# Two transformer blocks on one core: a ring of expert weights with 20 buffers instead of 18, and another order of its buffers and of the second block's first loads

## The chip, the core and the metric

The program runs on one core of a Trainium2 chip. Its time is device microseconds of one execution; the median of three runs of the kernel before is 1735.8 us (1735.76 to 1737.29). The engines of the core are TensorE (PE, with its weight loads shown as PEld), VectorE (DVE), ScalarE (ACT), GpSimd (POOL) and SyncE (SP), which here does little else than issue DMAs.

## The reference

256 tokens of width 1024 go through two blocks. The first projects the tokens, runs a causal convolution of width 31 and a gated linear attention, mixes both, and then a mixture of experts: a router takes one of 8 groups and two of its 8 experts for each token. The second block has four branches (a recurrent mixer, window means, a sparse attention, an attention over 256 memory tokens) and a gated feed-forward part. The part around the change is the mixture of experts:

```
e_logits = logits of the chosen group; top 2 of 8, softmax, times the group's weight
hdn = silu(xb @ w1[e]) * (xb @ w3[e])        # xb: the tokens of expert e, w1 and w3: 1024 x 512
y   = hdn @ w2[e]                            # w2: 512 x 1024
out = sum over the two experts of weight * y # 64 experts, f32 throughout
```

All 64 experts are computed, each for the tokens that chose it.

## The kernel before

Everything is one program, and a planner (the tile framework, with `schedule_with_timeline_sim=True`, L1681) writes the order of the instructions on each engine from a time that it simulates; in a few stretches the order of some engines is that of the source (`manual_schedule`). Weights come as pieces of 128 x 2048 f32, 1 MB or 8 KB a partition, all issued by SP in program order (L139).

*The first block* (`first`, `first_in`, `first_out`) reads its pieces through the pool `wp` of three buffers. ACT copies each piece to a rounded `hi` (L170), DVE and POOL compute the rest `lo` (L172, L173), and PE multiplies three times (L186 to L188). Its tiles that live long (gates, convolution, the pool `keep1`) lie on the right side of the memory.

*The experts* (`Experts`, `experts`) are computed in 32 pairs. A pair needs 12 pieces: w1 and w3 of both experts in halves (8), then w2 in halves (4). Two pieces for the memory tokens' keys and values come after pair 6 (`mem_at`). The class `Experts` deals the loads out over a ring of buffers that belong to several pools: `wq0` (3), `wq1` (3), `wp` (3), `lo` (3) and `wq2` (6), 18 in all; in the first round three buffers of `hi` come behind them, so 21 loads are issued before a buffer has to come back. A load waits until the last reader of its buffer is done; SP issues in order, so what stands behind it waits too. `wq0` and `wq1` open while the first block still runs, `wq2` when `keep1` is closed.

One pair (`block`) is: 32 gathers of the tokens with one-hot matrices (L786), one copy (L789), the product with w1 and w3 (L796, 64 instructions), a copy and four transposes (L799, L802), silu and product (L807, L808), the product with w2 (L815, 32), two copies and eight accumulating matmuls (L865). The gathers of the next pair do not depend on this one, and the planner mixes them into L815. Behind pair 3 stands a loop for experts with over 32 tokens (`overflow`), behind pair 6 the projection of the memory tokens (`memory_kv`). A small pool `mid` on the right side holds that projection's results.

*The second block* (`second`) starts with a layer norm of the experts' sum, which needs two rows of parameters (`ln2`, loaded into a `lo` buffer, read by L263 and L267) and a gain (`gain`, read by L1071). Its SP queue is written out (L1043 to L1053): one piece of weights, ln2, gain, two more pieces, then five tables. Tiles of this block lie on the right side, where `wq2` was.

Of the kernel before, what the change touches and what calls it, by code (L numbers as in the profile page):

```python
# [8 lines left out]
F32 = mybir.dt.float32  # L9
# [8 lines left out]
P = 128  # L18
T = 256
# [109 lines left out]
class Stream:  # L129


    def __init__(self, nc, pool):
        self.nc, self.pool = nc, pool
# [136 lines left out]
def first(tc, A, k):  # L270
    nc = tc.nc
    ps, x1, st = k.ps, k.x1, k.stream
    ident, ones = k.cav("ident"), k.cav("ones")
    V, S, G = nc.vector, nc.scalar, nc.gpsimd

    def bank(shape=(P, 512)):
        return ps.tile(list(shape), F32, tag="ps", name="pst", bufs=k.n_ps)

    def mx(shape=(P, 512)):
        return ps.tile(list(shape), F32, tag="mx", name="mxt", bufs=8 - k.n_ps)  # L280

    st.open([A["s1"][i] for i in range(A["s1"].shape[0])])
    sp = Split(nc, k.hi, k.lo)
    dn = Dense(k, sp, st.take, bank)
    tail = ExitStack()
    with ExitStack() as es:
        bp = es.enter_context(tc.tile_pool(name="keep1", bufs=1, side="right"))
        kept = {n: bp.tile([P, NB, T], F32, tag=n, name=n) for n in ("lk", "vn", "g1", "g0", "cv")}
        kept.update({n: bp.tile([P, NB, T], F32R, tag=n, name=n) for n in ("oh", "ol")})
        cols = bp.tile([P, NCOLS1], F32, name="cols")  # L290

        def col(name, j=0):
            return cols[:, COLS1[name][0] + j:COLS1[name][0] + j + 1]

        with ExitStack() as es2:
            tp = es2.enter_context(tc.tile_pool(name="tmp1", bufs=2, side="right"))
            ap = es2.enter_context(tc.tile_pool(name="act1", bufs=1, side="right"))
            early = es2.enter_context(ExitStack())
            first_in(tc, A, k, dn, sp, bank, mx, kept, cols, col, bp, ap, tp, early)
        sp.cut = PIECE * 5 // 8  # L300
        k.experts.open("wq1", k.n_q1)
        ap = tail.enter_context(tc.tile_pool(name="tail", reuse_waits="tile", bufs=1))
        rows = ap.tile([P, NROWS1 - 1536], F32, name="rows")
        nc.scalar.dma_start(rows[:], A["rows1"][:, 1536:].to_broadcast([P, NROWS1 - 1536]))
        wrt = ap.tile([P, NB, 72], F32, name="wrt")
        nc.scalar.dma_start(wrt[:], A["wrt"])

        def row(name):
            a, b = ROWS1[name]
            return rows[:, a - 1536:b - 1536]  # L310

        r = Route(tc, k, ap, mx, wrt, row("b_rt"))
        first_out(tc, A, k, dn, sp, bank, kept, col, row, bp, ap, r.logits)
    k.open_mid()
    k.experts.open("wq2", k.n_q2, "right")
    k.experts.ahead(k.experts.depth)
    with tail:
        r.choose()
# [402 lines left out]
class Experts:  # L721


    def __init__(self, tc, A, k, es):
        self.tc, self.k, self.es = tc, k, es
        self.w1, self.w3, self.w2 = A["w1"][0], A["w3"][0], A["w2"][0]
        loads = self.loads = []
        for pr in range(32):
            for kh in range(2):
                for e in (2 * pr, 2 * pr + 1):  # L730
                    loads += [(("1", e, kh), self.half(self.w1[e], kh)), (("3", e, kh), self.half(self.w3[e], kh))]
            for jh in range(2):
                for e in (2 * pr, 2 * pr + 1):
                    loads.append((("2", e, jh), self.half(self.w2[e], jh)))
            if pr == k.mem_at:
                loads += [(("m", 0, kh), A["wm"][kh]) for kh in range(2)]
        self.index = {key: i for i, (key, _) in enumerate(loads)}
        self.got, self.at = {}, 0
        self.pools = {"wp": k.wp, "lo": k.lo, "hi": k.hi}
        ring = ["wq0"] * k.n_q0 + ["wq1"] * k.n_q1 + ["wp"] * k.n_wp + ["lo"] * k.n_lo + ["wq2"] * k.n_q2  # L740
        self.depth = len(ring) + k.n_hi
        self.order = ring + ["hi"] * k.n_hi + ring * (len(loads) // len(ring))

# [270 lines left out]
def second(tc, A, k, out):  # L1014
    nc = tc.nc
# [5 lines left out]
    st_ = k.stream  # L1021
# [8 lines left out]
    with ExitStack() as es:  # L1030
# [12 lines left out]
        with tc.manual_schedule(engines={mybir.EngineType.SP}):  # L1043
            st_.ahead(1)
            ln2 = st_.load(A["rows2"][:, :2 * D].to_broadcast([P, 2 * D]), k.lo)
            ln2 = ln2[:].rearrange("p (a d) -> p a d", a=2)
            nc.sync.dma_start(gain[:], A["rows2"][:, 4 * D:5 * D].to_broadcast([P, D]))
            st_.ahead(3)
            nc.sync.dma_start(cr, A["const_h"].rearrange("p (a b) -> p a b", a=4))
            nc.sync.dma_start(cl[:], A["const_l"].rearrange("p (m t) -> p m t", m=7))  # L1050
            nc.sync.dma_start(cpm[:], A["const_p"])
            nc.sync.dma_start(cb[:], A["const_b"])
            nc.sync.dma_start(pw[:], A["pool_wl"])  # L1053
# [457 lines left out]
def body(tc, A, out):  # L1511
    nc = tc.nc
    k = K()
    k.n_hi, k.n_lo, k.n_wp, k.n_ps = 3, 3, 3, 4
    k.n_q0, k.n_q1, k.n_q2 = 3, 3, 6
    k.loop_at = 4
    k.mem_at = 6
    with ExitStack() as es:
        cp = es.enter_context(tc.tile_pool(name="const", bufs=1))
        k.hi = es.enter_context(tc.tile_pool(name="hi", bufs=k.n_hi))  # L1520
        k.lo = es.enter_context(tc.tile_pool(name="lo", bufs=k.n_lo))
        k.wp = es.enter_context(tc.tile_pool(name="wp", bufs=k.n_wp))
        k.ps = es.enter_context(tc.tile_pool(name="psum", bufs=4, space=PSUM))
        k.stream = Stream(nc, k.wp)
        k.ca = cp.tile([P, NCA], F32, name="ca")
        k.cav = lambda n: k.ca[:, CA[n][0]:CA[n][1]]
        k.eps_ln = cp.tile([P, 1], F32, name="eps_ln")
        k.eps_rms = cp.tile([P, 1], F32, name="eps_rms")
        nc.vector.memset(k.eps_ln[:], LN_EPS)
        nc.vector.memset(k.eps_rms[:], RMS_EPS)  # L1530
        k.x1 = cp.tile([P, 2, D], F32, name="x1")
        k.am = cp.tile([P, 2, 64], BF16, name="am")
        k.counts = cp.tile([P, 2, P], BF16, name="counts")
        k.W = cp.tile([P, 2, 64], F32, name="Wt")
        k.pos = cp.tile([P, 2, 64], F32, name="pos")
        k.ovn = cp.tile([P, 64], F32, name="ovn")
        k.ovs = cp.tile([P, 64], F32, name="ovs")
        k.n_extra = cp.tile([1, 1], I32, name="n_extra")
        k.count = cp.tile([P, 1], F32, name="count")
        k.cols2 = cp.tile([P, NCOLS2], F32, name="cols2")  # L1540
        k.col2 = lambda n, j=0: k.cols2[:, COLS2[n][0] + j:COLS2[n][0] + j + 1]
        nc.vector.memset(k.count[:], 0.0)
        with ExitStack() as mid:
            rings = mid.enter_context(ExitStack())

            def open_mid():
                pool = mid0.enter_context(tc.tile_pool(name="mid", reuse_waits="tile", bufs=1, side="right"))
                k.mid = pool
                k.mkT = pool.tile([P, 2, T], F32, name="mkT")
                k.mv = pool.tile([P, 2, T], F32, name="mv")  # L1550
                k.lb = pool.tile([P, 2, 4], F32, name="lb")
                k.lbm = pool.tile([P, 2, 4], F32, name="lbm")

            mid0 = es.enter_context(ExitStack())
            k.open_mid = open_mid
            k.experts = Experts(tc, A, k, rings)
            first(tc, A, k)
            nc.scalar.dma_start(k.cols2[:], A["cols2"])
            experts(tc, A, k)
        k.stream.open([A["s2"][i] for i in range(A["s2"].shape[0])])  # L1560
        second(tc, A, k, out)


# [121 lines left out]
```

## Time and profile before

| | |
|---|---|
| median of three runs | 1735.8 us |
| profiled execution | 1743.47 us, span 1741.7 us |
| PE busy | 1621.3 us, 93% |
| PEld busy | 1120.6 us, 64% |
| DVE, ACT, POOL busy | 553.3, 461.8, 491.9 us |
| moved by DMA | 533.20 MB, 306 GB/s over the span |
| expert loads | 384 of 1 MB, all issued by SP, 19.4 us median from issue to landing |

Engine busy times count the stretch from an instruction's start to its end; matmul ends are modelled. "Share" of the DMA is the mean over 16 DMA engines. PEclk is the clock that TensorE was granted, as a share of 2.4 GHz.

### The profile page before, as it was taken

To read this page: it belongs to the slowest core of one execution; us is meant where nothing else is said; L and a number is where in the kernel's file an instruction comes from. 1 tells how busy PE (TensorE), PEld (TensorE's weight loads), DVE (VectorE), ACT (ScalarE), POOL (GpSimd) and SP (SyncE) were. 2 spreads that over 40 slices of the span, in tenths; PEclk is the share of its full clock that TensorE was granted. 3 is DMA by queue.
4 is the path that set the end of the run, shared out by engine and by line. 5 is a ranking of instruction groups with operands and counts; after the bars stand their busy time and mean duration, and the time that the engine had idled before them with its cause. 6 is when DMAs were issued, how large, how long until landed. Compare 5 with 4: busy or idle time off the path is not lost. (4 is left out here: it accounts for less than half of the span.)

```text
span 1741.7 us, 23653 instructions
## 1 busy us (share of the span) xinstructions
PE 1621.3 (93%) x9895; PEld 1120.6 (64%) x9895; DVE 553.3 (32%) x1034; ACT 461.8 (27%) x618; POOL 491.9 (28%) x338
## 2 busy tenths in 40 slices
PE   8999998999899999999999999999699998979998
PEld 7999995445455444444354434444399997979997
DVE  5888684110110000000000000000563866453233
ACT  6445751100200000000000000000356544454333
POOL 6767742000000000000000000000354454556664
PEclk9999996898898997787877787787899998989999
DMA  7453678999989999999999999999544332535551
GB/s 272 162 181 140 250 282 326 426 412 425 426 365 417 426 427 426 426 426 426 426 426 426 426 426 426 426 426 416 190 155 161 113 131 97 182 121 191 177 188 73
DMA packets 75694, 533.20 MB, mean 306 GB/s; under 512 B 8497, under 2 KB 9009, under 8 KB 11970
## 3 DMA queue, kind: packets, MB, share of 16 engines
q1 hardware_dynamic: 74178, 526.61, 74.7%
q10 hardware_dynamic: 1408, 5.06, 0.7%
q8 instruction: 79, 1.29, 0.3%
q14 instruction: 29, 0.24, 0.0%
HBM read 530.59 MB, written 1.05 MB: 305 GB/s over the span
## 5 line engine op out<-in xcount | busy, mean ns | idle before, releaser
L173 POOL TENSOR_TENSOR lo<-w,hi 128x768 fp32r<-128x768 f32 (+2 forms) x112 | 379.2, 3391 | 353.6 <-ACT hi L170 253.7
L786 PEld LDWEIGHTS pst<-S,x 128*128 128x128 f32 x1024 | 249.3, 334 | 80.1 <-issue 78.7
L170 ACT ACTIVATE hi<-w 128x2048 fp32r<-128x2048 f32 (+1 forms) x112 | 208.9, 1868 | 224.1 <-PE pst L187 123.1
L796 PE MATMUL pst<-w,xe 128*32 128x512 f32 x2048 | 267.3, 612 | 1.1 <-DVE xe L789 1.1
L815 PE MATMUL pst<-w,hd 128*32 128x512 f32 x1024 | 245.6, 893 | 24.4 <-DVE hd L808 24.4
L841 POOL TENSOR_TENSOR sw<-S,Wt 128x64 f32<-128x64 f32 x128 | 33.3, 292 | 827.3 <-DVE S L851 546.4
L786 PE MATMUL pst<-S,x 128*128 128x64 f32 x1024 | 261.3, 421 | 1.5 <-DVE S L851 1.2
L187 PE MATMUL pst<-ul,hi 128*128 128x256 f32 x768 | 218.4, 285 | 0.0
L188 PE MATMUL pst<-uh,lo 128*128 128x256 f32 x768 | 217.9, 285 | 0.3 <-DVE lo L172 0.3
L186 PE MATMUL pst<-uh,hi 128*128 128x256 f32 x768 | 217.5, 284 | 0.0
L796 PEld LDWEIGHTS pst<-w,xe 128*32 128x32 f32 x2048 | 70.3, 113 | 167.2 <-issue 160.0
L172 DVE TENSOR_TENSOR lo<-w,hi 128x1280 fp32r<-128x1280 f32 (+1 forms) x78 | 124.4, 1595 | 157.0 <-ACT hi L170 148.7
L186 PEld LDWEIGHTS pst<-uh,hi 128*128 128x128 f32 x768 | 145.9, 190 | 1.7 <-ACT il L1152 0.3
L188 PEld LDWEIGHTS pst<-uh,lo 128*128 128x128 f32 x768 | 145.0, 189 | 2.1 <-DVE lo L172 0.9
L187 PEld LDWEIGHTS pst<-ul,hi 128*128 128x128 f32 x768 | 145.1, 189 | 1.8 <-issue 0.5
L808 DVE TENSOR_TENSOR hd<-si,pst 128x128 f32<-128x128 f32 x64 | 18.5, 288 | 377.6 <-ACT si L807 377.6
L789 DVE COPY xe<-pst 128x512 f32<-128x512 f32 x32 | 22.1, 692 | 340.2 <-PE pst L786 340.2
L815 PEld LDWEIGHTS pst<-w,hd 128*32 128x32 f32 x1024 | 42.3, 141 | 120.1 <-issue 80.1
L845 ACT ACTIVATE WT<-pst 128x256 f32<-128x256 f32 x32 | 12.3, 384 | 400.5 <-PE pst L843 383.9
L368 DVE SCALAR_TENSOR_TENSOR mxt<-U,cols,mxt 128x256 f32<-128x256 f32 x232 | 113.2, 488 | 6.9
L865 PE MATMUL acc<-ys,WT 64*128 64x512 f32 x256 | 89.2, 694 | 16.4 <-DVE ys L823 16.4
L186 PE MATMUL pst<-xh,hi 128*128 128x256 f32 x352 | 98.8, 284 | 6.1 <-ACT hi L170 6.0
(399 smaller groups left out, 2054.9 us busy)
## 6 DMA issues: line engine op xcount, KB each, us to landing
w<-in_w_dram SPq DMA_DIRECT2D x384, 1024.0 KB, 19.4
w<-in_s_dram SPq DMA_DIRECT2D x108, 1024.0 KB, 4.8
w<-in_wm_dram SPq DMA_DIRECT2D x2, 1024.0 KB, 19.5
rows<-in_rows_dram ACTq DMA_DIRECT2D x1, 1572.0 KB
w<-in_s_dram SPq DMA_DIRECT2D x4, 256.0 KB, 6.7
xn<-in_x_dram ACTq DMA_DIRECT2D x1, 1024.0 KB, 9.0
mem<-in_mem_dram ACTq DMA_DIRECT2D x1, 1024.0 KB, 11.2
w<-in_rows_dram SPq DMA_DIRECT2D x1, 1024.0 KB, 9.1
```

Source lines behind the costliest of these rows:

```text
L170: nc.scalar.activation(hi[:, s], raw[:, s], AF.Copy)
L172: nc.vector.tensor_tensor(lo[:, v], raw[:, v], hf[:, v], op=OP.subtract)
L173: nc.gpsimd.tensor_tensor(lo[:, g], raw[:, g], hf[:, g], op=OP.subtract)
L186: mm(out, lh, rh, start=start and c == 0, stop=False, skip_group_check=True)
L187: mm(out, lh, rl, start=False, stop=False, skip_group_check=True)
L188: mm(out, ll, rh, start=False, stop=stop and c == n - 1, skip_group_check=True)
L368: V.scalar_tensor_tensor(cv[:, blk] if j == 30 else acc, U[:, blk, j:j + T], cols[:, cw + j:cw + j + 1], acc, op0=OP.mult, op1=OP.add)
L786: nc.tensor.matmul(pg[:, c], x1[:, t, c::NB], Sx[:, t], start=t == 0, stop=t == 1)
L796: nc.tensor.matmul(ph[g:g + 32, :], xe[:, c, e * CAP:(e + 1) * CAP], w[:, c % 4, :], start=c == 0, stop=c == NB - 1)
L815: nc.tensor.matmul(py[g:g + 32, :], hd[:, j, e], w[:, j % 2, half * 512:half * 512 + 512], start=j == 0, stop=j == 3)
L841: G.tensor_tensor(sw[:, t, dup, :m].rearrange("p (e s) -> p e s", e=n), Sx[:, t].rearrange("p (e s) -> p e s", e=n), wts[t], op=OP.mult)
L865: nc.tensor.matmul(acc[t][half][:], wt_, y, start=pr == 0, stop=pr == 31, skip_group_check=True)
```

## The change

The ring has 20 buffers. `wq2` has eight instead of six, and four of them stand ahead of `wp` and `lo` in the order of the ring, so that 23 loads are issued in the first round. The place in memory comes from the scratch kept for dynamic DMAs, which is set to 1024 bytes, and the four tiles of the pool `mid` go into the constants' pool; `open_mid` goes away. In the second block's SP queue two pieces of weights are issued ahead of the gain instead of behind it.

```diff
-    k.open_mid()
     k.experts.open("wq2", k.n_q2, "right")
...
-        ring = ["wq0"] * k.n_q0 + ["wq1"] * k.n_q1 + ["wp"] * k.n_wp + ["lo"] * k.n_lo + ["wq2"] * k.n_q2
+        ring = (["wq0"] * k.n_q0 + ["wq1"] * k.n_q1 + ["wq2"] * 4 + ["wp"] * k.n_wp + ["lo"] * k.n_lo
+                + ["wq2"] * (k.n_q2 - 4))
         self.depth = len(ring) + k.n_hi
...
+            st_.ahead(3)
             nc.sync.dma_start(gain[:], A["rows2"][:, 4 * D:5 * D].to_broadcast([P, D]))
-            st_.ahead(3)
...
-    k.n_q0, k.n_q1, k.n_q2 = 3, 3, 6
+    k.n_q0, k.n_q1, k.n_q2 = 3, 3, 8
...
+        k.mkT = cp.tile([P, 2, T], F32, name="mkT")
+        k.mv = cp.tile([P, 2, T], F32, name="mv")
+        k.lb = cp.tile([P, 2, 4], F32, name="lb")
+        k.lbm = cp.tile([P, 2, 4], F32, name="lbm")
...
-    nc = bacc.Bacc("TRN2", target_bir_lowering=False, num_devices=1)
+    nc = bacc.Bacc("TRN2", target_bir_lowering=False, num_devices=1, dynamic_dma_scratch_size=1024)
```

## Rows read from the trace of the kernel before

**Rows 1.** The page: the span, and GB/s moved in 40 equal slices.

```profile
span 1741.7 us, 23653 instructions
...
GB/s 272 162 181 140 250 282 326 426 412 425 426 365 417 426 427 426 426 426 426 426 426 426 426 426 426 426 426 416 190 155 161 113 131 97 182 121 191 177 188 73
```

**Rows 2.** Windows by pair: start:end, length, busy by engine (count), PEclk, DMA share, GB/s.

```profile
358.60:383.90 25.30, 23.73 (x146) 12.36 (x142) 2.41 (x6) 2.13 (x5) 1.04 (x4) 0.93 1.01 425
...
415.90:444.30 28.40, 26.05 (x142) 13.14 (x142) 4.54 (x14) 6.45 (x16) 1.04 (x4) 0.94 1.01 426
...
520.30:550.80 30.50, 27.77 (x142) 13.27 (x142) 2.22 (x6) 2.13 (x5) 1.04 (x4) 0.83 1.00 414
550.80:575.00 24.20, 22.69 (x142) 12.18 (x142) 2.22 (x6) 2.13 (x5) 1.04 (x4) 1.00 1.01 426
...
599.30:627.80 28.50, 26.21 (x142) 13.14 (x142) 2.22 (x6) 2.13 (x5) 1.04 (x4) 0.88 1.01 424
...
656.20:687.00 30.80, 28.48 (x142) 13.82 (x142) 2.22 (x6) 2.13 (x5) 1.04 (x4) 0.72 1.01 426
...
656.20:1195.60 539.40, 501.30 (x2556) 239.84 (x2556) 39.66 (x106) 38.31 (x90) 17.74 (x68) 0.79 1.01 426
```

**Rows 3.** Waits of PEld, whole span: line, releaser, us in total, times, longest.

```profile
PEld pst L796 <- DMA w<-in_w_dram: 4.2, 8, 1.1
...
PEld pst L815 <- DMA w<-in_w_dram: 1.2, 4, 0.3
```

**Rows 4.** Waits of the SP queue, whole span.

```profile
SPq L139 <- DMA w<-in_w_dram: 475.8, 249, 2.8
...
SPq L139 <- PE pst L796: 175.0, 59, 19.4
```

**Rows 5.** Windows, columns as in rows 2: stretches in which the DMA slows down.

```profile
250.00:262.00 12.00, 12.00 (x61) 10.03 (x60) 9.05 (x11) 5.62 (x5) 6.21 (x2) 1.00 0.57 186
...
292.00:302.00 10.00, 9.64 (x52) 4.78 (x55) 0.96 (x3) 0.38 (x1) 1.04 (x4) 0.57 0.39 162
...
510.00:515.00 5.00, 4.64 (x23) 1.10 (x26) 0.96 (x3) 0.38 (x1) 1.04 (x4) 0.50 0.48 198
515.00:520.00 5.00, 5.00 (x48) 1.28 (x40) 0.00 (x0) 0.00 (x0) 0.00 (x0) 0.94 0.42 125
```

**Rows 6.** Timeline of PE in a pair of 24.2 us: start, us, instruction.

```profile
558.47 1.92 PE L815 MATMUL pst<-w,hd 128*32 128x512 f32 x16
560.33 1.16 PE L786 MATMUL pst<-S,x 128*128 128x64 f32 x4
```

**Rows 7.** Timeline of PE in a pair of 30.8 us.

```profile
663.90 3.64 PE L815 MATMUL pst<-w,hd 128*32 128x512 f32 x16
667.48 3.60 PE L786 MATMUL pst<-S,x 128*128 128x64 f32 x14
```

**Rows 8.** Timeline of DVE at the end of the first block.

```profile
258.48 2.06 DVE L179 TENSOR_TENSOR ml<-g,mh 128x256 fp32r<-128x256 f32 x1
```

**Rows 9.** Timeline of PE: the first expert product.

```profile
296.01 9.32 PE L796 MATMUL pst<-w,xe 128*32 128x512 f32 x64 [0.35 <-DVE xe L789]
```

**Rows 10.** Timeline of the SP queue where the second block begins.

```profile
1214.43 0.33 SPq L139 DMA_DIRECT2D w<-in_rows_dram  x1
1232.11 0.33 SPq L1047 DMA_DIRECT2D gain<-in_rows_dram  x1
```

**Rows 11.** Timeline of all engines there.

```profile
1219.17 7.07 PE L796 MATMUL pst<-w,xe 128*32 128x512 f32 x62
...
1236.31 1.41 DVE L263 SCALAR_TENSOR_TENSOR x<-acc,lmv,w 128x512 f32<-128x512 f32 x2
...
1244.47 1.97 PE L1010 MATMUL mxt<-ca,un 128*128 128x128 f32 x8 [8.32 <-DVE un L1071]
...
1252.67 3.90 DVE L1000 TENSOR_TENSOR rss<-rss 128x1 f32<-128x1 f32 x1 [0.79 <-ACT un L994]
```

**Rows 12.** DMA issues: queue, count, KB, median us to landing.

```profile
w<-in_rows_dram SPq DMA_DIRECT2D x1, 1024.0 KB, 9.1
```

More of the change, by code (lines that the diff above doesn't have):

```diff
@@ L1542, in body @@
         nc.vector.memset(k.count[:], 0.0)
+        k.mkT = cp.tile([P, 2, T], F32, name="mkT")
+        k.mv = cp.tile([P, 2, T], F32, name="mv")
+        k.lb = cp.tile([P, 2, 4], F32, name="lb")
+        k.lbm = cp.tile([P, 2, 4], F32, name="lbm")
         with ExitStack() as mid:
             rings = mid.enter_context(ExitStack())
[L1546 to L1555, printed above, removed]
             k.experts = Experts(tc, A, k, rings)
```

## The prediction

> **What bounds the kernel now.** I read the page's span and DMA rate by slices first: from the eighth to the 28th of 40 slices the rate stands at 412 to 427 GB/s, and once at 365 [rows 1]. That is the expert stage, 384 loads of 1 MB. So I asked next for the same stage pair by pair, from the end of one pair's L796 to the end of the next's [rows 2] (they are pairs 3, 5, 8, 9, 11 and 13, and the 18 pairs from 13 to 30). The reader is to see two things that do not fit together at first sight: the DMA share is 1.01, and PE is busy 501.30 of 539.40 us. Twelve loads of 1.0486 MB at 426 GB/s need 29.5 us; the 18 pairs took 539.4 / 18 = 29.97 us each. Both look full. The waits decide: over the whole kernel the expert matmuls' weight loads waited 4.2 + 1.2 us for a DMA, in 12 spells of at most 1.1 us [rows 3]. PE therefore does not stand waiting for weights; it paces itself. SP for its part waits mostly for an earlier DMA (475.8 us, 249 times) and less for a buffer (175.0 us for L796) [rows 4].
>
> Why does PE need 29.97 us? Some pairs take 24.2 us at a granted clock of 1.00, that is the upper level of 2.4 GHz, others 28.4 to 30.8 us at a mean of 0.72 to 0.94, part of the time at 1.2 GHz [rows 2]. The instructions are the same 142; their order is not. In the quick pair the second block of L815 follows after 4 gathers (L786, 1.16 us), and 16 L815 take 1.92 us. In the slow pair all 14 gathers stand in one piece (3.60 us) and 16 L815 take 3.64 us [rows 6, 7]. The order is written by the planner from its own simulated time. My reading, argued and not shown by a row: it fills in gathers where it believes that L815 must wait for the pair's last w2 weights. So a weight that comes earlier in the planner's time moves the order on PE, although PE never waits for it on the chip.
>
> **The change, part by part.** Durations are of the profiled execution (1743.47 us, span 1741.7); the sum is a difference, carried over to the median of 1735.8, which is 7.7 us lower.
>
> Two more buffers (ring 20 instead of 18, first fill 23 loads instead of 21). Two loads are 2 x 1.0486 MB / 426 GB/s = 4.9 us of feed. They count only where the ring was full and the DMA stood still. This is so twice. After the first fill, 292 to 302 us, the rate is 162 GB/s: 10 x (1 - 162/426) = 6.2 us lost. While PE does the memory projection of pair 6, 510 to 520 us, it is 198 and 125: 2.7 + 3.5 = 6.2 us lost [rows 5]. Each stall ends when PE gives a buffer back, so each can return at most 4.9 us: the feed is 4.9 us ahead after the first and at most 9.8 us after the second. At PE itself the direct worth lies between 0 and the 5.4 us of waits [rows 3]; I take 0, since 12 spells of 0.45 us on average in 32 pairs are no sign of weights that come late.
>
> What is left is the order. I take one pair ahead of the memory projection to become a quicker one: 28.4 us against the 25.3 of an earlier pair, and to be careful two thirds of the difference: 0.67 x 3.1 = 2.1 us. And one pair after the memory projection: 30.5 us in the first, 28.5 in the fourth, mean 29.5, against 24.2: 5.3 us [rows 2]. Sum 7.4 us. It stays under the 9.8 us of feed, so PE would not run out of weights. The lower end is 0 (the order stays), the upper 2 x 3.1 + 6.3 + 4.3 = 16.8 us if two pairs turn on each side; from the 656 us mark on I leave the pace at 29.97 us.
>
> The ring's order. Four wq2 loads move ahead of wp and lo. They lie on memory of the first block's tiles, the gates among them, whose last reader is DVE's L179 at 258.48 + 2.06 = 260.5 us [rows 8]. SP issues in order, so the three wp and three lo loads may queue behind that wait, some 10 us later than before. It costs nothing as long as the first expert matmul starts at 296.01 us [rows 9]: from 260.5 the DMA can bring (296.0 - 260.5) / 2.46 = 14 loads, and pair 0 wants 12, of which six are there before. The gain: 250 to 262 us runs at 186 GB/s, 6.8 us unused [rows 5], which the moved loads fill; without it the two new loads might not land before 302 us.
>
> The scratch. 16 KB a partition are needed; 4 KB of tiles only move to the constants and the rest comes from the scratch. Every issue in the list of DMAs stands on SP's or ACT's queue, of which one row is shown [rows 12], so nobody should miss it: 0.
>
> The second block's loads. The last loads now fall otherwise on the buffers: the ln2 rows take the lo buffer of pair 31's third load, read in the first half of the last L796 (1219.17 + 7.07), so ln2 is issued near 1222.8 instead of 1214.43 us. Behind it on SP stand two weight pieces, the gain rows and five tables; the gain no longer waits for the last L815 (1232.11 us before), so they leave some 9 us earlier [rows 10, 11]. ln2 took 9.1 us to land [rows 12]: 1231.9 us, and DVE's L263, which first reads it, starts at 1236.31. Cover 4.4 us. PE then waits for DVE, 8.32 us up to 1244.47, and no load is in that chain [rows 11]. So 0; bounds: were ln2 to wait for the last L815, 1232.1 + 9.1 - 1236.3 = +4.9 us. Below nothing: tables that land earlier may let POOL take its splits in another order, and one DVE addition on 128x1, in PE's chain, took 3.90 us beside such a split [rows 11]: at most -3.9 us. I stay at 0, nearest to the wait that no load sets.
>
> **Rivals.** *Hidden anyway (B):* the planner leaves the order, PE paces itself, the DMA only waits longer with a fuller ring. For it: 5.4 us of waits in all [rows 3]. Against: the order does differ between early and late pairs. Time 1735.8 us.
>
> *The feed is the bound after all (C):* PE's pace follows the weights by more than the rows of waits tell, and all lost DMA time comes back, 4.9 + 6.2 = 11.1 us: 1724.7 us; down to 1719 with the upper end of 16.8. For it: a share of 1.01 for the whole stretch. Against: PE had only (539.4 - 501.3) / 18 = 2.1 us of idle a pair, all of it behind ACT and DVE. The Trainium skill's page "Perfetto Trace Analysis", section "Identifying the Most-Contended Engine", bears on this: it holds matmul busy time a poor measure of headroom and would judge PE by its weight loads. By that rule PE (239.84 of 539.40 us, 44%) has room and the DMA is the bound, which is this rival. The trace agrees as to the DMA share and not as to the waits.
>
> *Slower (D):* a better feed reshuffles the order of the long steady stretch. Pair 13 took 30.8 us at clock 0.72 [rows 2]. If all 20 pairs from 12 on took that, 20 x (30.8 - 29.97) = +16.6 us, less 7.4: 1745.0 us. It decides from a mean of 29.97 + 7.4 / 20 = 30.34 us a pair. For it: the clock falls with small changes of order. Against: in the long stretch the planner thinks itself short of weights with either ring, so that two buffers should not alter it.
>
> *It doesn't do what it says (E):* the scratch is needed, or the fill is not earlier; as B in time.
>
> **How the numbers follow.** What a measurement can tell from no change is about 0.2%, 3.5 us. Forecast A, 1735.8 - 7.4 = 1728.4 us, own range 1724 to 1732: 0.48. B and E 0.22 (same). C 0.15 (faster). D 0.15 (slower). Faster 0.63, same 0.22, slower 0.15. The range leaves out some of C and nearly all of D: 1718 to 1740 us.
>
> **What would show it.** The buffers: 23 expert loads ahead of the first stall, and less DMA time lost near 510 us. The order: one or two more pairs of 24 to 26 us at clock 1.00 before the steady stretch, and its pace still 29.9 us. If the feed comes earlier and the pairs take what they took, B is right. If pairs late in the stage take under 29 us, C; over 30.3, D. The transition: gain issued before 1232 us on the old clock of events, PE's wait for DVE still about 8.3 us; a wait of DVE for ln2 would prove that step wrong.

## The result, and the profile after

The changed kernel is slower: 1746.9 us (1744.6 to 1749.3, four runs) against 1735.8 us (1735.0 to 1737.3), ratio 1.0063 with a 95% interval of 1.0045 to 1.0080. Ten runs of it in all have a median of 1747.4 us, 147 runs of the kernel before, beside it and the experiments, one of 1737.7 us: 9.7 us. Single runs of the kernel before lie anywhere from 1731.3 to 1744.0 us; the profiled one, at 1743.47, was a slow draw, the profiled one of the changed kernel (1749.26) too. Medians are compared below, and traces for where the time lies.

The page of the changed kernel: span, granted clock and GB/s by slices.

```profile
span 1747.4 us, 23639 instructions
...
PEclk9999996898898988687887887787899998989999
...
GB/s 262 171 179 133 250 272 379 417 412 419 420 376 416 420 420 420 421 420 420 421 420 420 421 420 420 420 420 405 226 146 158 113 140 97 181 121 185 179 190 73
```

The steady rate of the feed is 420 GB/s, and 426 before [rows 1]. The windows of the changed kernel: the pairs of [rows 2] with pair 6 among them, then pairs 9 to 12 in one, then the stretches of [rows 5], the last of them cut finer (columns as there: length, busy by engine, PEclk, DMA share, GB/s):

```profile
361.00:386.20 25.20, 23.66 (x143) 12.34 (x142) 2.41 (x6) 2.13 (x5) 1.05 (x4) 0.93 1.01 423
418.20:446.60 28.40, 26.06 (x146) 13.13 (x142) 4.54 (x14) 6.45 (x16) 1.04 (x4) 0.94 1.02 419
446.60:476.10 29.50, 26.70 (x142) 13.03 (x142) 2.29 (x7) 3.41 (x6) 1.05 (x4) 0.83 1.01 420
523.30:553.70 30.40, 27.70 (x142) 13.23 (x142) 2.22 (x6) 2.13 (x5) 1.04 (x4) 0.83 1.00 413
553.70:579.70 26.00, 24.46 (x144) 12.34 (x142) 2.22 (x6) 2.13 (x5) 1.04 (x4) 0.87 1.01 421
605.10:633.60 28.50, 26.21 (x142) 13.13 (x142) 2.22 (x6) 2.13 (x5) 1.05 (x4) 0.88 1.01 420
661.90:692.70 30.80, 28.52 (x145) 13.84 (x142) 2.22 (x6) 2.13 (x5) 1.04 (x4) 0.72 1.01 421
661.90:1201.40 539.50, 501.35 (x2559) 239.74 (x2556) 39.68 (x106) 38.31 (x90) 17.73 (x68) 0.79 1.01 420
...
553.70:661.90 108.20, 101.28 (x570) 50.98 (x568) 8.88 (x24) 8.52 (x20) 4.18 (x16) 0.89 1.01 420
...
250.00:262.00 12.00, 12.00 (x65) 10.23 (x64) 10.15 (x14) 6.45 (x7) 5.47 (x2) 1.00 0.38 113
292.00:302.00 10.00, 9.65 (x44) 6.85 (x47) 0.96 (x3) 0.38 (x1) 1.33 (x6) 0.50 1.01 421
...
510.00:515.00 5.00, 4.65 (x22) 4.00 (x25) 0.96 (x3) 0.38 (x1) 0.23 (x1) 0.61 1.01 415
515.00:517.50 2.50, 2.50 (x16) 0.59 (x12) 0.00 (x0) 0.00 (x0) 0.81 (x4) 0.50 0.77 321
517.50:520.00 2.50, 2.50 (x24) 0.61 (x20) 0.00 (x0) 0.00 (x0) 0.00 (x0) 0.91 0.03 10
520.00:522.50 2.50, 2.50 (x28) 0.71 (x24) 0.00 (x0) 0.00 (x0) 0.00 (x0) 1.00 0.67 164
```

Windows of the kernel before that were not shown, pair 6 and pairs 9 to 12:

```profile
444.30:472.40 28.10, 26.15 (x142) 13.00 (x142) 2.29 (x7) 3.41 (x6) 1.04 (x4) 0.82 1.01 427
...
550.80:656.20 105.40, 98.50 (x568) 50.67 (x568) 8.87 (x24) 8.51 (x20) 4.18 (x16) 0.94 1.01 426
```

The reader is to see four things. The feed did what was meant only in part. From 292 to 302 us it runs at 421 GB/s, where it stood half still before [rows 5]. But the stall behind the memory projection is still there, some 5 us later: from 515 to 522.5 us 4.6 us of feed are lost (2.5 us each at 321, 10 and 164 of 420 GB/s), for 6.2 us before. The steady stretch of 18 pairs takes 539.5 us, as before. Pair 6 takes 29.5 instead of 28.1 us, and pairs 9 to 12 take 108.2 instead of 105.4 us at a mean clock of 0.89 instead of 0.94. And no pair became quicker by more than 0.7 us (pair 7).

PE's waits for weights, and SP's (columns as in [rows 3, 4]):

```profile
PEld pst L796 <- DMA w<-in_w_dram: 3.6, 12, 0.3
```

```profile
SPq L139 <- DMA w<-in_w_dram: 548.5, 276, 2.7
...
SPq L139 <- PE pst L796: 135.3, 49, 15.2
```

SP waits less for a buffer (135.3 for 175.0 us) and more for earlier DMAs. PE's waits for weights fell from 5.4 to 3.6 us. That is the whole direct gain of two buffers.

Where the time of the traces lies, by stretch (from the starts and ends of L796 and the span). The last five rows are experiments that come below: f2 is the kernel before with the small scratch alone; h2 is the changed kernel with 64 unused bytes ahead of the first block's tiles on the right, h3 with 64 more ahead of the second block's, i1 is h3 with the ring of 18, and h4 the kernel before with 128 unused bytes.

| us | to the first L796 | pairs 0-3 | 4-5 | 6 | 7-12 | 13-31 | rest |
|---|---|---|---|---|---|---|---|
| before, the profiled run | 296.0 | 87.9 | 60.4 | 28.1 | 183.8 | 570.0 | 515.5 |
| before, another (1732.0 us) | 292.4 | 83.2 | 60.5 | 28.1 | 180.5 | 570.1 | 515.5 |
| after | 298.8 | 87.4 | 60.4 | 29.5 | 185.9 | 570.0 | 515.4 |
| f2 | 296.2 | 87.4 | 60.4 | 28.1 | 189.3 | 567.9 | 515.4 |
| h2 | 290.8 | 82.1 | 67.6 | 31.4 | 185.7 | 567.8 | 515.4 |
| h3 | 290.9 | 84.8 | 64.3 | 31.4 | 185.7 | 567.8 | 508.3 |
| i1 | 290.0 | 83.2 | 60.6 | 28.0 | 189.5 | 567.9 | 508.3 |
| h4 | 293.4 | 83.2 | 60.6 | 28.0 | 182.8 | 567.8 | 508.3 |

The first two rows are the same program: 11.5 us between them lie ahead of pair 13, in stretches whose clock fell more often in one than in the other. That is the scatter against which everything below has to be read. Between the profiled runs of before and after the 5.7 us are 2.8 in the first block, 1.3 in pair 6, 2.1 in pairs 7 to 12, and -0.5 in pairs 0 to 3.

### The profile page after: what moved, and what is told of

Same layout as the page of the kernel before. It is cut to its first block, busy times and chain, and to the rows that moved or that the text cites. A ratio compares the mean times of both kernels' runs of the same rounds, so it can differ in the third digit from the quotient of the medians.

```text
span 1747.4 us, 23639 instructions
## 1 busy us (share of the span) xinstructions
PE 1625.7 (93%) x9895; PEld 1123.5 (64%) x9895; DVE 553.3 (32%) x1034; ACT 461.5 (26%) x618; POOL 492.3 (28%) x338
## 3 DMA queue, kind: packets, MB, share of 16 engines
HBM read 530.59 MB, written 1.05 MB: 304 GB/s over the span
## 5 line engine op out<-in xcount | busy, mean ns | idle before, releaser
L815 PE MATMUL pst<-w,hd 128*32 128x512 f32 x1024 | 249.2, 902 | 24.4 <-DVE hd L808 24.4
L796 PE MATMUL pst<-w,xe 128*32 128x512 f32 x2048 | 265.5, 610 | 1.1 <-DVE xe L789 1.1
L188 PE MATMUL pst<-uh,lo 128*128 128x256 f32 x768 | 217.8, 284 | 0.3 <-DVE lo L172 0.3
L186 PE MATMUL pst<-uh,hi 128*128 128x256 f32 x768 | 217.3, 284 | 0.0
L796 PEld LDWEIGHTS pst<-w,xe 128*32 128x32 f32 x2048 | 70.0, 112 | 166.3 <-issue 160.4
L186 PEld LDWEIGHTS pst<-uh,hi 128*128 128x128 f32 x768 | 146.2, 191 | 1.7 <-ACT il L1152 0.3
L188 PEld LDWEIGHTS pst<-uh,lo 128*128 128x128 f32 x768 | 145.1, 189 | 2.1 <-DVE lo L172 0.9
L815 PEld LDWEIGHTS pst<-w,hd 128*32 128x32 f32 x1024 | 42.6, 142 | 121.3 <-issue 82.3
L186 PE MATMUL pst<-xh,hi 128*128 128x256 f32 x352 | 99.8, 287 | 6.7 <-ACT hi L170 6.7
L865 PE MATMUL acc<-ys,WT 64*128 64x512 f32 x256 | 89.7, 695 | 17.2 <-DVE ys L823 17.2
```

Source lines behind the costliest of these rows:

```text
L186: mm(out, lh, rh, start=start and c == 0, stop=False, skip_group_check=True)
L188: mm(out, ll, rh, start=False, stop=stop and c == n - 1, skip_group_check=True)
L796: nc.tensor.matmul(ph[g:g + 32, :], xe[:, c, e * CAP:(e + 1) * CAP], w[:, c % 4, :], start=c == 0, stop=c == NB - 1)
L815: nc.tensor.matmul(py[g:g + 32, :], hd[:, j, e], w[:, j % 2, half * 512:half * 512 + 512], start=j == 0, stop=j == 3)
L865: nc.tensor.matmul(acc[t][half][:], wt_, y, start=pr == 0, stop=pr == 31, skip_group_check=True)
```

## Experiments: the parts of the change (e1 to e4)

The layout alone, then with the second block's load order, then with eight wq2 buffers in the old order, then with the new order of the ring.

```diff
+        k.mkT = cp.tile([P, 2, T], F32, name="mkT")
...
+    nc = bacc.Bacc("TRN2", target_bir_lowering=False, num_devices=1, dynamic_dma_scratch_size=1024)
...
+            st_.ahead(3)                                  # e2 alone: ahead of the gain
...
+    k.n_q0, k.n_q1, k.n_q2 = 3, 3, 8                      # e3, e4
...
+        ring = (["wq0"] * k.n_q0 + ["wq1"] * k.n_q1 + ["wq2"] * 4 + ["wp"] * k.n_wp   # e4
```

Expected of e1: 

> Scratch of 1024 bytes and the four tiles among the constants, with the ring of 18 in its old order and the old load order. Theory R (rate): the new place of the tiles or the small scratch slows the loads themselves, which in the profile after run at 420 instead of 426 GB/s; then this kernel is already about 11 us slower (1747) and shows 420 GB/s. Theory O (order and clock): the time went because the ring moved the order of PE's work and with it the clock that PE is granted; then this kernel is as fast as before, 1734 to 1738 us, with the order of PE's work of before. Theory S (second block): the load order there costs it; then also as before.

Expected of e2: 

> As the layout run, and two weight pieces ahead of the gain in the second block's queue. Theory S: about 1746 us. Theories O and R: the same as the layout run within 2 us, since the wait of PE for DVE at the start of the second block (8.3 us) does not hang on these loads.

Expected of e3: 

> Ring of 20 in the old order of buffers (all eight of the new pool at its end), old load order in the second block. Theory O: slower than before if pair 6 or pairs 9 and 10 lose their order or clock, 1739 to 1747 us; if it stays at 1736 then the new order of the buffers, not their number, is to blame. Theory R: 1747 us as the layout run. My forecast's own reading (two loads more give earlier weights) would have it at 1728 us.

Expected of e4: 

> The whole change but the second block's load order. Theory S: as before, 1736 us. Theories O and R: as the changed kernel, 1745 to 1749 us, with pairs 9 and 10 of 25 to 26 us instead of 24.2 us.

| | median us | ratio to before | pair 6 |
|---|---|---|---|
| e1 layout | 1742.9 | 1.0041 (1.0023 to 1.0060) | 28.1 |
| e2 and the load order | 1741.4 | 1.0031 (1.0012 to 1.0050) | 28.1 |
| e3 layout, ring of 20 | 1747.9 | 1.0061 (1.0037 to 1.0085) | 31.4 |
| e4 and the ring's order | 1746.6 | 1.0057 (1.0034 to 1.0079) | 31.4 |

The second block's load order and the ring's order cost nothing that can be told. The layout (the small scratch and the moved tiles) costs some 5 us, though every instruction of e1 stands on its engine as in the kernel before, and the ring of 20 here 5 more. All four feed at 420 GB/s, so e1 spoke for the theory that the slower feed costs the time, if with less than its 1747 us. That theory did not last.

## Experiments: the place in memory (f1 to f4)

```diff
+    ... num_devices=1, dynamic_dma_scratch_size=1024)          # f2, nothing else
...
+        k.pad = cp.tile([P, 112], F32, name="pad")             # f3: e1 with 448 bytes
...
+        k.pad = cp.tile([P, 16], F32, name="pad")              # f4: before with 64 bytes
```

Expected of f1: 

> The kernel before, unchanged. Of the rate of the expert loads (mean of their 8 KB packets between 600 and 1180 us: 309.8 ns before, 314.4 ns in the changed kernel and in all four kernels with its layout) three theories are open. Theory P, the place of the ring in SBUF (a tile of 64 bytes that moved into the constants shifts three quarters of the ring's buffers by 64 bytes): 309.8 ns here, about 1737 us. Theory C, the size of the scratch (1 KB instead of 16 KB): the same here. Theory N, the chip on which a run falls, and not the kernel: 314 ns here too, 420 GB/s in the slices.

Expected of f2: 

> The kernel before with the scratch of 1 KB alone: every tile on the left stands 15,360 bytes lower, a multiple of 512, and nothing else differs. Theory P: 309.8 ns and 1737 us, no change. Theory C: 314.4 ns and the 4 to 6 us that the layout cost, 1742 us. Theory N: 314 ns, as the kernel before on this chip.

Expected of f3: 

> The changed kernel's layout (scratch of 1 KB, the mid tiles in the constants) with the ring, its order and the second block's loads as before, and 448 unused bytes more in the constants, so that the left buffers of the ring start on multiples of 512 again; the right ones stand at 480 past such a multiple. Theory P: 309.8 ns, 1737 us. Theory C and theory N: 314 ns, 1742 us by C.

Expected of f4: 

> The kernel before with 64 unused bytes in the constants, so that the left buffers of the ring start 64 bytes past a multiple of 512; scratch and mid tiles as before. Theory P: 314.4 ns and 1741 to 1743 us. Theory C: 309.8 ns, 1737 us. Theory N: as the kernel before on this chip.

Their 8 KB packets took, in the mean, 309.8 ns in f1 and f2, 310.3 in f3, 314.0 in f4. So the feed follows the place of the ring's left buffers (64 bytes past a multiple of 512 in e1 and f4), as theory P has it, and neither the scratch's size nor the chip. But the times: f1 1739.1 us (ratio 1.0011, 0.9989 to 1.0032), f2 1741.5 (1.0016, 0.9997 to 1.0036), f3 1740.5 (1.0006, 0.9988 to 1.0024), and f4 1732.9 (0.9962, 0.9941 to 0.9983). The kernel with the slow feed is the fastest: the expectation of f4 failed, and the theory of the feed with it. The page of f4, GB/s by slices, is that of a slow feed, and its 18 steady pairs take 539.5 us, as in the kernel before. Below it are the 18 steady pairs of e1 and of f2, which have PE's order in common: 420 and 426 GB/s, and 537.3 us in both. The feed does not set the pace.

```profile
GB/s 275 159 181 128 250 275 337 405 412 420 421 381 414 421 421 421 422 421 421 422 421 421 422 421 422 421 421 421 290 146 171 122 123 120 163 132 182 191 194 73
```

```profile
658.60:1195.90 537.30, 499.17 (x2559) 238.98 (x2556) 39.66 (x106) 38.31 (x90) 17.81 (x68) 0.80 1.01 420
```

```profile
661.50:1198.80 537.30, 499.18 (x2556) 239.25 (x2556) 39.63 (x106) 38.27 (x90) 17.74 (x68) 0.80 1.01 426
```

Where did f4 win? In the second block (508.3 us after pair 31, 515.5 in the kernel before), where no expert load runs. So I looked at PE itself: the time from one 128x256 matmul of the dense layers (L186 to L188) to the next, at a granted clock of 1.00. The same run of 184 matmuls, its first and last start, in the kernel before, the changed one, and h2 (below):

```profile
51.46 0.28 PE L186 MATMUL pst<-xh,hi 128*128 128x256 f32 x1
...
73.01 0.28 PE L187 MATMUL pst<-xl,hi 128*128 128x256 f32 x1
```

```profile
51.32 0.28 PE L186 MATMUL pst<-xh,hi 128*128 128x256 f32 x1
...
73.27 0.28 PE L187 MATMUL pst<-xl,hi 128*128 128x256 f32 x1
```

```profile
51.16 0.28 PE L186 MATMUL pst<-xh,hi 128*128 128x256 f32 x1
...
71.92 0.28 PE L187 MATMUL pst<-xl,hi 128*128 128x256 f32 x1
```

Over 183 steps that is 117.8, 120.0 and 113.5 ns. Nothing stands between these matmuls in any of the three. What differs is where their operands start ("moving" are the 256 columns that run through, "weights" the 128x128 tile that is loaded first; start addresses in the built programs, modulo 128; means of the steps under 180 ns at full clock, some 1010 in the first block and some 2220 in the second):

| moving operand, weights | difference | where | ns |
|---|---|---|---|
| 64, 64 | 0 | first block of after, e1, f4 | 119.7 |
| 64, 0 | 64 | first block of before, f2, f3 | 117.4 |
| 0, 64 | 64 | first block of h2 to h4 | 115.5 |
| 96, 0 and 32, 64 | 96 | second block of before, and of after and e1 | 119.9 |
| 32, 0 | 32 | second block of f3, g3 | 117.9 |
| 96, 64 | 32 | second block of f4, h3, h4 | 116.9 |

The four small tiles of `mid` that moved into the constants take 4,160 bytes a partition, so everything behind them on the left, `hi` and `lo` among it, shifted by 64 bytes modulo 128, and the first block's steps went from 117.4 to 119.7 ns: 1010 x 2.3 ns = 2.3 us, with 376 more of the same form (117.7 to 119.9 ns) 3.1 us. This is theory M of the last experiments. For f4 the steps give 2220 x 3.0 ns less 3.1 us, 3.6 us of gain; the medians gave 7.4, and the other 3.8 us are not explained.

## Experiments: the ring without the shift, and another order (g1 to g4)

```diff
+    k.n_q0, k.n_q1, k.n_q2 = 3, 3, 7                            # g1: f2 with 7; g2: with 8
...
+        k.pad = cp.tile([P, 112], F32, name="pad")              # g3: after with 448 bytes
...
+        late = ring + ["wq2"] * 2                               # g4: f2, 8 buffers in wq2
+        self.order = ring + ["hi"] * k.n_hi + ring * 5 + late * (len(loads) // len(late))
```

Expected of g1: 

> The kernel before with the scratch of 1 KB and seven wq2 buffers, a ring of 19: one load more ahead, and the order of the instructions on PE, DVE, ACT and POOL is word for word that of the kernel before. Theory O (the ring costs time because the planner, with 20 buffers, writes pair 6 in another order, 28.1 us turning into 29.5 to 31.4, and the clock falls otherwise behind it): as the scratch alone, 1741 us within 3. Theory F (more loads in flight cost by themselves): half of the ring's 5 us, 1743 to 1744. Theory A, the one of my prediction (a load that comes earlier saves time): under 1739.

Expected of g2: 

> As the one before, with eight wq2 buffers, a ring of 20 in the old order; the mid tiles stay where they were, so that the ring's buffers start on the same places (modulo 512) as in the kernel before. On PE ten instructions of pair 6 stand elsewhere, else nothing. Theory O: pair 6 at 29.5 us or over and the whole at 1746 us, 3 to 6 over the ring of 19. Theory F: 1746 too, but without a longer pair 6. If the place of the buffers were what made the changed kernel slow: 1738 to 1741.

Expected of g3: 

> The changed kernel with 448 unused bytes in the constants, so that the left buffers of its ring start on multiples of 512 as in the kernel before. Theory R (the slower feed of 420 GB/s costs the time): packets of 310 to 311 ns, 426 GB/s, and some 5 us back, 1742 us. Theory O (order and clock, the feed is off the path): the rate comes back and the time stays at 1744 to 1749.

Expected of g4: 

> The scratch of 1 KB and eight wq2 buffers of which the first six rounds take six a round and the later ones eight. The planner writes pairs 5 to 10 in another order, most with L815 in one piece of 28 (as in the pairs of the start that took 25.3 us). Theory A of my prediction (such pairs are quicker): 3 us less in at least three pairs, under 1735. Theory O without a direction (any other order draws the clock anew): between 1730 and 1750, and the pairs whose order differs are those whose length differs.

Measured: g1 1741.2 us (ratio 1.0025, 1.0008 to 1.0041), g2 1742.9 (1.0027, 1.0009 to 1.0044), g3 1738.7 (1.0002, 0.9986 to 1.0019), g4 1743.8 (1.0037, 1.0021 to 1.0053). In g2 pair 6 took 31.4 us as theory O has it, but the whole was only 1.7 us over g1, not 3 to 6: inconclusive, within the scatter. g3 met neither theory as I had put them: the time came back, more than theory R had it. But with the feed (310.0 ns) the operands came back too (512.4 us after pair 31 and the steps of the table), so g3 cannot part the two; h3 below does. g4 missed theory A: of its turned pairs, pair 6 took 25.6 us, the very form that I had hoped for, and pair 9 took 30.3. Turning the order moves single pairs by several us in either direction.

f2 and g1 say something more, of the scratch. f2 alone shows no difference that can be told. But g1 is slower clear of no change, though PE's order, its operands' places and the feed are those of the kernel before, and i2 against i1 below shows nothing for the one load more. No run of f2 or g1 is under 1738.2 us; 82 of the 147 runs of the kernel before are. In the traces of all seven kernels with the small scratch and PE's old order (e1, e2, f2, f3, g1, i1, i2) pairs 7 to 31 take 757.2 to 757.4 us, in the four with the large scratch (before, f1, f4, h4) 750.6 to 753.9. So the small scratch, or the place 15,360 bytes lower that comes with it, seems to cost 1 to 4 us (by medians 1.3 in f2 and 3.6 in g1 over the kernel before beside them, 1.2 in i1 over h4). How is not shown. From f4 to f2, which have PE's order in common, the first difference of time behind pair 3 is one wait of PE for `hd` in pair 7, which is *shorter* in f2; from there on the clock falls in other places. The same wait is 1.05 us in all four and 0.75 in all seven. First f4, then f2:

```profile
525.13 1.05 PE L815 MATMUL pst<-w,hd 128*32 128x512 f32 x4 [1.05 <-DVE hd L808]
```

```profile
522.40 1.05 PE L815 MATMUL pst<-w,hd 128*32 128x512 f32 x4 [0.75 <-DVE hd L808]
```

The order of pair 6 in the kernel before and, below, in the changed kernel (timeline of PE: start, us, instruction, count):

```profile
453.00 3.64 PE L815 MATMUL pst<-w,hd 128*32 128x512 f32 x16
456.58 3.55 PE L786 MATMUL pst<-S,x 128*128 128x64 f32 x14
460.06 1.91 PE L815 MATMUL pst<-w,hd 128*32 128x512 f32 x12
```

```profile
455.31 3.63 PE L815 MATMUL pst<-w,hd 128*32 128x512 f32 x12
458.87 3.54 PE L786 MATMUL pst<-S,x 128*128 128x64 f32 x14
462.25 0.28 PE L843 MATMUL pst<-ca,sw 128*128 128x128 f32 x1
462.45 1.05 PE L815 MATMUL pst<-w,hd 128*32 128x512 f32 x4
463.44 0.33 PE L843 MATMUL pst<-ca,sw 128*128 128x128 f32 x1
463.70 1.91 PE L815 MATMUL pst<-w,hd 128*32 128x512 f32 x12
```

Twelve L815 take 3.63 us where sixteen took 3.64, four more take 1.05 us behind an L843, and L865 and the next L796 start that much later. In the built program and in the trace it is the only pair whose order on PE the ring of 20 turned.

## Experiments: operands and ring told apart (h1 to h4, i1, i2)

```diff
+        es.enter_context(tc.tile_pool(name="sh1", bufs=1, side="right")).tile([P, 16], F32, name="sh1")  # h2, h3, h4, i1, i2: ahead of keep1
         bp = es.enter_context(tc.tile_pool(name="keep1", bufs=1, side="right"))
...
+        es.enter_context(tc.tile_pool(name="sh2", bufs=1, side="right")).tile([P, 16], F32, name="sh2")  # h3, i1, i2: ahead of act2
...
+    k.n_q0, k.n_q1, k.n_q2 = 3, 3, 6                            # i1; 7 in i2
```

Expected of h1: 

> The changed kernel, unchanged, beside the three others. All theories: 1744 to 1749 us; its first block at full clock gives 119.7 ns from one of the 128x256 matmuls (L186 to L188) to the next.

Expected of h2: 

> The changed kernel with 64 unused bytes ahead of the first block's right pools (keep1, tmp1, act1), so that the operands of its 128x256 matmuls lie 64 and 32 bytes apart modulo 128 again, as in the kernel before, and not 0 and 96. The order of every engine, the ring and the feed are those of the changed kernel. Theory M (the cadence of PE's matmuls depends on how the moving operand lies against the weights, modulo 128): 117.4 instead of 119.7 ns in the first block, 1040 x 2.2 + 376 x 2.1 = 3.1 us, so 1743 to 1744 us; the feed stays at 420 GB/s. Rival N (a shifted tile only draws the clock anew): the cadence stays at 119.7 ns, the time is anything from 1735 to 1750. Rival R (the slower feed costs the time): no change, 1747.

Expected of h3: 

> As the one before, with 64 unused bytes ahead of the second block's right pools too, so that its 2217 matmuls of this form have their operands 32 bytes apart instead of 96. Theory M: 116.9 instead of 119.9 ns there, 6.6 us more, so 1736 to 1738 us, with the feed still at 420 GB/s. Rival N: cadence as before. Rival R: 1747.

Expected of h4: 

> The kernel before with 64 unused bytes in the constants (which gave 1732.9 us) and the 64 bytes ahead of the first block's right pools: 64 and 32 bytes apart in the first block, 32 in the second. Theory M: 3.1 us under 1732.9, so 1730 us within 2, 7 to 9 under the kernel before. Rival N: 1727 to 1745. Rival R: 1741 or more, as the feed is at 420 GB/s.

Expected of i1: 

> The changed kernel with both 64-byte shifts (which gave 1735.0 us) and six wq2 buffers again: a ring of 18, scratch, mid tiles and load orders as in the changed kernel. PE's order is that of the kernel before. Theory O (the ring costs time through the order of pair 6 and the clock around it): pair 6 at 28.1 us, pairs 4 and 5 at 60.4 us, 1730 us within 2, as the kernel before with its two shifts (1730.3). Rival P (what is left comes from the scratch and the other places): 1735.

Expected of i2: 

> The same with seven wq2 buffers, a ring of 19: one load more ahead, PE's order still that of the kernel before. Theory O: as with six, 1730 us within 2, pair 6 at 28.1 us. Rival F (loads in flight cost by themselves): half of the 4.7 us between the rings of 18 and 20, 1732.5 us. Rival P: 1735. Theory A of my prediction (a load that comes earlier saves time at PE): under 1728.

| | median us | ratio to before | feed |
|---|---|---|---|
| h1, the changed kernel | 1747.7 | 1.0046 (1.0028 to 1.0064) | 420 |
| h2, first block's operands moved | 1742.3 | 1.0022 (1.0007 to 1.0037) | 420 |
| h3, the second block's too | 1735.0 | 0.9975 (0.9963 to 0.9987) | 420 |
| h4, before, with both | 1730.3 | 0.9946 (0.9920 to 0.9972) | 421 |
| i1, h3 with a ring of 18 | 1731.5 | 0.9966 (0.9950 to 0.9983) | 420 |
| i2, h3 with a ring of 19 | 1731.6 | 0.9958 (0.9939 to 0.9977) | 420 |

h2 and h3 change no instruction's place on any engine. h2 gave 5.4 us back where 3.1 were expected, because the steps fell to 115.5 and not to 117.4 ns: 1010 x 4.2 + 376 x 2.6 ns = 5.2 us. h3 gave 7.3 us more where 6.6 were expected. Its second block, a run of 96 matmuls, in the changed kernel and in h3 (120.0 and 116.7 ns over 95 steps):

```profile
1579.05 0.28 PE L186 MATMUL pst<-uh,hi 128*128 128x256 f32 x1
...
1590.45 0.28 PE L188 MATMUL pst<-uh,lo 128*128 128x256 f32 x1
```

```profile
1567.81 0.28 PE L186 MATMUL pst<-uh,hi 128*128 128x256 f32 x1
...
1578.90 0.27 PE L188 MATMUL pst<-uh,lo 128*128 128x256 f32 x1
```

h3, with the feed at 420 GB/s, refutes theory R. h4 met its number, in part by luck: by the steps it should lie 5.4 us under f4 and not the 3.1 that I had put, and it lies 2.6 under. i1 and i2 keep the layout, its places and both load orders: with a ring of 18 or 19, under which PE's order is that of the kernel before, the time is 1731.5 us, and the ring of 20 (h3) takes 3.5 more. Its trace has 3.7 us more than i1's in pairs 4 and 5, 3.4 more in pair 6, and 3.8 less in pairs 7 to 12. The ring's cost is not one number, though: 5.0 us by e3 and e1, 3.5 by h3 and i1, 1.7 by g2 and g1, and nothing by g3 and f3 (1.0002 and 1.0006 of the kernel before). What all ring-of-20 traces in the planner's turned order share is a pair 6 of 29.5 to 31.4 us instead of 28.1. The windows of pair 6 in h3, i1, i2 and g4:

```profile
440.00:471.40 31.40, 28.64 (x142) 13.24 (x142) 2.28 (x7) 3.41 (x6) 1.04 (x4) 0.78 1.01 419
```

```profile
433.80:461.80 28.00, 26.05 (x142) 12.99 (x142) 2.29 (x7) 3.41 (x6) 1.05 (x4) 0.82 1.01 420
```

```profile
438.40:466.60 28.20, 26.20 (x145) 13.00 (x142) 2.29 (x7) 3.41 (x6) 1.04 (x4) 0.82 1.01 419
```

```profile
443.70:469.30 25.60, 23.65 (x142) 12.35 (x142) 2.29 (x7) 3.41 (x6) 1.04 (x4) 0.93 1.01 427
```

A load that is ahead costs nothing that can be told by itself (i2 against i1), and is worth nothing by itself. h4 beats both kernels: the kernel before, with 128 unused bytes a partition.

## Why the prediction was wrong, by its steps

*What bounds the kernel* was right: PE paces itself. At 420 GB/s twelve loads need 30.0 us, as long as a pair takes, and the pace is the same to 0.1 us in 539.4; e1 and f2 show it again, at 537.3. So was the steady pace (29.97 us a pair), and so was the direct worth of the feed (0; PE's waits fell by 1.8 us). Of the second stall less came back than the 4.9 us at most that I allowed (4.6 us lost for 6.2), and rival C's sum counted all 6.2 of it, against that same bound; neither touched the forecast.

*The order* is the step that failed first. I took one pair ahead of the memory projection and one behind it to turn quicker, 2.1 + 5.3 us. One pair turned, the sixth, and it became longer, by 1.3 us in the profiled run and 3.3 in h3; none behind it turned. My reading of a quick and a slow pair was of single instances: the length came with the granted clock, and nothing in the rows said in which direction a turned order moves it. Pairs 9 to 12 kept their order, and the clock fell elsewhere in them. In place of the 7.4 us that this term was to save, the ring of 20 cost between nothing and 5.0 us in four pairs of kernels.

*The scratch* is the second. I looked for who misses the scratch and wrote 0, and had not asked what the tiles' new addresses do. By the steps of PE they cost the first block 3.1 us, and h2 shows that moving the operands away again gives that time back, and more, while the feed stays slow. Whether the scratch itself costs nothing is open: f2 alone cannot tell it, g1 says 3.6 us.

*The second block's loads* were right, and e2 shows it. The SP queue of the changed kernel there, which answers to [rows 10]:

```profile
1228.56 0.33 SPq L139 DMA_DIRECT2D w<-in_rows_dram  x1
1228.94 0.90 SPq L139 DMA_DIRECT2D w<-in_s_dram  x2
1229.88 0.55 SPq L1048 DMA_DIRECT2D gain<-in_rows_dram  x1
1241.33 0.33 SPq L1049 DMA_DIRECT2D il<-in_const_h_dram  x1
```

Less the 5.8 us by which PE is late there, ln2 goes out at 1222.8 as forecast, and the gain at 1224.1. The tables do not leave earlier, they wait until 1241.33: that detail was wrong, and free, for PE waits for DVE as long as before [rows 11]:

```profile
1250.20 1.11 PE L1010 MATMUL mxt<-ca,un 128*128 128x128 f32 x4 [8.32 <-DVE un L1071]
```

*The ring's order*: nothing, right. The filling at 250 to 262 us that I counted on did not come (113 GB/s, 186 before), since wq2's first loads wait where wp's had gone out; by e4 against e3 it cost nothing that can be told.

*Rival D* came out near in time (1745.0 us) and is refuted in its mechanism: the steady stretch did not move. No rival of mine had the place of the operands.

*What stays open*: of the 9.7 us, 3.1 are shown in PE's steps. The rest is shared by the ring (nothing to 5.0 us) and the small scratch with its lower place (1 to 4 us), both of which show in pairs 4 to 31, and I have not separated them: there the profiled run of the changed kernel and f2, with the old ring, both take 845.8 us, the kernel before 842.4. Nor is it settled why the clock of pairs 4 and 5, whose order is unchanged, was lower in h2 and h3 (67.6 and 64.3 us for 60.6), or why the feed slows with the place of its buffers.

## What to carry to other kernels

A change that only makes room moves every tile behind it: compare the start addresses of PE's operands modulo 128 before and after, and measure the step from matmul to matmul in one long run at full clock, before blaming the ring that was made. Where PE paces itself, an earlier load is worth what PE's waits for it add up to, and a planner that sees it may turn an order for the worse; here a buffer less (19 for 20) kept the order. When one program scatters by 12 us, a profile of one run prices nothing under that; stretches at one clock do.

## What the runs showed of the hardware

The step of a 128x256 matmul depends on where its moving operand lies against its weights: 115.5 to 117.9 ns in the mean where they start 32 or 64 bytes apart modulo 128, 119.7 to 119.9 ns where they start 0 or 96 apart, in seven combinations from two blocks. The distance is not all of it: at the same distance the steps with weights that start at 64 are shorter than with weights at 0 (115.5 for 117.4 ns, 116.9 for 117.9). The Trainium skill, "TensorE: Matmul & The Clock Gate", section "Wait — 56ns, not 53.3ns?", has one spacing for warm matmuls, the columns at 2.4 GHz and about 2.5 ns; for 256 columns that is an estimate of 109 ns. The trace does not agree: the lowest run here is 113.5 ns, the highest 120.0. Here each matmul has a weight load of its own (9895 of either on the page).

The 8 KB packets of the feed rose from 309.8 to 314 ns in the mean, when the left buffers started 64 bytes past a multiple of 512: between 600 and 1180 us 93% of them took 309 ns in the kernel before, 8% in the changed one, so it was not the left buffers' packets alone. The wq2 buffers lie off such a multiple in every kernel (416 bytes past one in the kernel before). The Trainium skill, "DMA: Bandwidth & Descriptors", section "How a descriptor splits into AXI transactions", has the first transaction of a descriptor that does not start on 256 bytes begin at the boundary below, at the cost of more beats. If that held for the places written here, which the page does not say, the wq2 loads of the kernel before should have been slow as well, a third of its ring; with 93% at 309 ns the rule does not explain it.
